# Two-layer hybrid encoder: seven-product pairs behind both standard parts, their products in another order, and two weight tiles a round split by an accumulating DMA

## The chip, the cores and the metric

One NeuronCore of one Trainium2 chip runs the whole program. The metric is device time in microseconds (us) from launch to end of one execution, lower is better. The kernel before takes 2075.16 us (median of 3 runs, 2074.29 to 2076.41).

## The reference, cut to what matters

```
SEQ, D_MODEL, D_FF, DEPTH = 256, 2048, 8192, 2           # batch 1, float32
for i in range(DEPTH):
    if i % 2 == 0: x = x + concat(conv(u), pool(u)) @ ev_w_out     # u = rms_norm(x) @ ev_w_in
    else:          x = x + fourier_mix(rms_norm(x)) @ od_w_out
    h = rms_norm(x, mlp_norm[i])
    x = x + jnp.square(jax.nn.relu(h @ mlp_w1[i])) @ mlp_w2[i]      # 2048 -> 8192 -> 2048
    g = jax.nn.sigmoid(rms_norm(x, ple_norm[i]) @ ple_w_gate[i])
    x = x + g * (p[i] @ ple_w_proj[i])
return rms_norm(x, final_norm)
```

The change lies in the line with `mlp_w1` and `mlp_w2` and in the order in which the products of `ple_w_gate` are added up.

## The kernel before, in words

**Split weights.** Every float32 product is made of three passes of a reduced-precision product: a value is held as hi + lo, and hi·hi, hi·lo and lo·hi are added up in PSUM (`PASSES_W_MOVES`). So every weight tile (128 x 2048 float32, 1 MB) is loaded by SyncE's queue into a buffer `raw` (4 of them), ScalarE writes its hi half into a buffer `hl` (L105), and VectorE writes lo = raw - hi beside it (L106). There are 4 `hl` buffers, used in turn, so the tile with number n can be split only when TensorE is through with the tile n-4. `Weights` holds the list of tiles in the order of their use; `run_ahead` splits up to three tiles ahead of the one in use. TensorE's and SyncE's instructions stand in the order in which the program names them; those of ScalarE and VectorE are ordered when the program is built, by a scheduler with priorities, and each engine then runs its own list strictly in that order.

**The MLP** (`mlp`, once a layer) goes in 8 rounds f. In each, `w1(q)` makes one block of 512 hidden columns from 4 tiles: of each tile it first does all products with the hi half (L580, 16 matmuls of 512 columns), then all with the lo half (L585, 16 of 256 columns). Its result is put through relu and square, split into `h` (L595 to L600) and combined into the sums `g` (L605 to L612). `w2(f, n)` is a standard product of two hidden blocks with two tiles of output columns n, added to x at its end (L366). `pair(f)` does the other half of the second product, output columns 0 to 1023, with seven products instead of eight (a Strassen-like scheme): for each of two blocks q the weights are two tiles, x and y, whose halves are split as they are or after an addition in place on VectorE (L102). The 14 products, each with 1024 columns of an `hl` tile, make 7 tiles; product by product they go into PSUM tiles a, b, c (1024 wide) and d (512), which VectorE adds to `sums` and to x (L649, L655, L657). After the last round `pair_end` combines `sums` into x (L662).

The order on TensorE in a round is w1(2f+2), w2(f,2), pair(f), w1(2f+3), w2(f,3); in the last round there is no w1, and `after.chunk(c)` brings parts of x, transposed by TensorE (L323) and split by ScalarE and VectorE (L262, L267), to the gate product that follows (`embed`, L345 with `ps_g`). `chunk` puts its transposes off by four steps of TensorE's work (`put_off`, `tick`).

The lines that set the order of the seven products before (weights, in `add_seven`):

```
parts += [
    [("split", (x, 0))], [("split", (x, q))],
    [("add", (x, 0), (y, 0)), ("split", (y, q))], [("split", (x, 0))],
    [("add", (y, 0), (y, q)), ("split", (y, 0))], [("add", (x, 0), (y, q)), ("split", (x, 0))],
    [("add", (x, 0), (x, q)), ("split", (x, 0))]]
```

Of the kernel before, what the change touches and what calls it, by code (L numbers as in the profile page):

```python
# [11 lines left out]
F32 = mybir.dt.float32  # L12
# [6 lines left out]
P = 128  # L19
# [11 lines left out]
RAW_BUFS = 4  # L31
RSQRT_MAGIC = float(0x5F3759DF)
# [10 lines left out]
class Weights:  # L43

# [24 lines left out]
    def add_seven(self, tiles):  # L69


        q, parts = 1024, []
        for x, y in tiles:
            x, y = self.source(x), self.source(y)
            parts += [
                [("split", (x, 0))], [("split", (x, q))],
                [("add", (x, 0), (y, 0)), ("split", (y, q))], [("split", (x, 0))],
                [("add", (y, 0), (y, q)), ("split", (y, 0))], [("add", (x, 0), (y, q)), ("split", (x, 0))],
                [("add", (x, 0), (x, q)), ("split", (x, 0))]]
# [15 lines left out]
    def divide(self, after_first=None):  # L95
# [3 lines left out]
        for i, (what, (r, c), other, w) in enumerate(steps):  # L99
# [6 lines left out]
            getattr(self.nc, lo).tensor_tensor(hl[:, 1, to], src, hl[:, 0, to].bitcast(F32), ALU.subtract)  # L106
# [32 lines left out]
def encoder(ctx: ExitStack, tc: tile.TileContext, a, out: bass.AP):  # L139
# [35 lines left out]
    def add_mlp(i):  # L175
        def w1(q):
            for c in range(4):
                ws.add(a["mlp_w1"][i, q, c])
# [102 lines left out]
    class Norm:  # L281
# [35 lines left out]
        def chunk(self, c):  # L317
# [9 lines left out]
            put_off(lambda: self.scale(c, turned))  # L327
# [228 lines left out]
    def mlp(i, norm, after):  # L556
# [64 lines left out]
        def pair(f):  # L621


            p15, p76, p23 = psum_mm(f"ps_s{i}_{f}a"), None, psum_mm(f"ps_s{i}_{f}b")
            p4 = sm_pool.tile([P, 512], F32, tag="sm", name=f"ps_s{i}_{f}d")
            k = 0
            for q in (2 * f, 2 * f + 1):
                h, g = hidden[q], forms[q]
                for what in range(7):
                    if k % 2 == 0:  # L630
                        w = ws.next()
                    if what == 4 and p76 is None:
                        p76 = psum_mm(f"ps_s{i}_{f}c")
                    out_ps = (lambda: p15[:, :512], lambda: p23[:, :512], lambda: p23[:, 512:], lambda: p15[:, 512:],
                              lambda: p76[:, :512], lambda: p76[:, 512:], lambda: p4)[what]()
                    for kt in range(2):
                        for m, (s, j) in enumerate(PASSES_W_MOVES):
                            act = (h[:, s, kt, :P], h[:, s, 2 + kt, :P], g[:, s, 3, kt], g[:, s, 0, kt],
                                   g[:, s, 2, kt], g[:, s, 1, kt], h[:, s, 2 + kt, P:])[what]
# [293 lines left out]
```

## Time and profile before

| | |
|---|---|
| median of 3 runs | 2075.16 us (2074.29 to 2076.41) |
| the profiled execution, its own time | 2070.65 us |
| its span, first to last instruction | 2068.9 us |
| mean granted clock of TensorE | 0.975 of full speed |
| TensorE, matmuls | 1977.0 us busy, 96% of the span |
| VectorE | 1564.3 us, 76% |
| ScalarE | 1039.6 us, 50% |
| GpSimd | 128.9 us, 6%, nearly all in the first layer's mixer |
| DMA | 377 MB, 182 GB/s over the span |

Shares of the span are averages over stages with different limits: the first 250 us are the mixer of layer 0, the two MLPs lie at about 252 to 990 us and 1213 to 1952 us, each followed by its gate product. Matmuls are pipelined and their ends are modelled, so TensorE's busy time counts some waiting; its pace is read from the starts of its instructions. PE is TensorE, DVE VectorE, ACT ScalarE, POOL GpSimd, SP SyncE; L106 is line 106 of the kernel.

### The profile page before, as it was taken

The numbers are of one execution on the slowest core, as the hardware profiler recorded it, in microseconds if no ns is written. First come the engines' busy times: TensorE is split into PE (matmuls) and PEld (weight loads), VectorE is DVE, ScalarE is ACT, GpSimd is POOL, SyncE is SP. The second block draws the span as 40 slices with busy tenths as digits, with TensorE's granted clock in tenths as the row PEclk, the third lists the DMA queues.
The fourth block names the chain that finished last, engine by engine and source line by source line (L and its number), as shares of the span: only waits on it lengthen the run. The fifth ranks groups of instructions, "written<-read, shape, count | busy, mean of one in ns | idle before, by whom it ended". The sixth has DMA issues, their size and how long they took to land.

```text
span 2068.9 us, 24040 instructions
## 1 busy us (share of the span) xinstructions
PE 1977.0 (96%) x9730; PEld 1668.3 (81%) x9730; DVE 1564.3 (76%) x1771; ACT 1039.6 (50%) x1087; POOL 128.9 (6%) x65
## 2 busy tenths in 40 slices
PE   8999999999999999998999999999999999999798
PEld 6888887878787787877789888787787878788686
DVE  7888768687787868779556567787868778787854
ACT  6345555445444545455454455545545445554543
POOL 3874000000000000000001000000000000000000
PEclk9999999999999999999999999999999999999999
DMA  8545554554536454464453554536364454635542
GB/s 330 192 170 191 206 188 168 187 203 143 224 140 227 152 214 183 143 223 162 152 183 135 183 183 146 224 139 240 137 231 169 159 209 146 222 135 203 182 164 108
DMA packets 55664, 377.43 MB, mean 182 GB/s; under 512 B 6384, under 2 KB 6528, under 8 KB 11648
## 3 DMA queue, kind: packets, MB, share of 16 engines
q1 hardware_dynamic: 55152, 374.82, 49.7%
q8 instruction: 76, 1.25, 0.2%
q10 hardware_dynamic: 144, 1.05, 0.1%
q14 instruction: 36, 0.29, 0.0%
q0 software_dynamic: 256, 0.02, 0.0%
HBM read 373.75 MB, written 2.10 MB: 182 GB/s over the span
## 4 chain that ended last, share of the span: by engine, by line
PE 69%; DVE 27%; issue 2%; ACT 2%; DMA 0%; ACTq 0%; SPq 0%
PE ps_h L580 21%; DVE hl L106 14%; PE ps_h L585 11%; PE ps_o L345 9%; PE ps_g L345 8%; DVE raw L102 7%; PE ps_od L345 4%; PE ps_in L345 4%; PE ps_out L345 3%; PE ps_pool L345 2%; ACT hl L105 2%; PE ps_outp L345 1%; PE ps_e L345 1%; DVE h L600 1%; DVE g L612 1%
## 5 line engine op out<-in xcount | busy, mean ns | idle before, releaser
L105 ACT ACTIVATE hl<-raw 128x2048 fp32r<-128x2048 f32 (+2 forms) x529 | 774.7, 1491 | 769.0 <-PE ps_h L585 315.8
L106 DVE TENSOR_TENSOR hl<-raw,hl 128x2048 fp32r<-128x2048 f32 (+3 forms) x501 | 865.5, 1744 | 381.5 <-ACT hl L105 379.8
L580 PE MATMUL ps_h<-xT_mlp,hl 128*128 128x512 f32 x2048 | 503.6, 399 | 0.0
L580 PEld LDWEIGHTS ps_h<-xT_mlp,hl 128*128 128x128 f32 x2048 | 391.1, 194 | 80.4
L345 PE MATMUL ps_o<-hl,h 128*128 128x512 f32 x1536 | 356.3, 391 | 0.0
L345 PEld LDWEIGHTS ps_o<-hl,h 128*128 128x128 f32 x1536 | 288.0, 189 | 58.7
L585 PEld LDWEIGHTS ps_h<-xT_mlp,hl 128*128 128x128 f32 x2048 | 262.6, 191 | 10.0
L585 PE MATMUL ps_h<-xT_mlp,hl 128*128 128x256 f32 x2048 | 266.0, 283 | 0.0
L345 PE MATMUL ps_g<-hl,xT_ple 128*128 128x512 f32 (+1 forms) x816 | 177.6, 377 | 0.0
L345 PEld LDWEIGHTS ps_g<-hl,xT_ple 128*128 128x128 f32 x816 | 146.4, 188 | 28.2 <-DVE hl L106 0.4
L106 POOL TENSOR_TENSOR hl<-raw,hl 128x2048 fp32r<-128x2048 f32 (+1 forms) x28 | 120.8, 4328 | 55.8 <-ACT hl L105 55.8
L345 PE MATMUL ps_in<-hl,xT_ev 128*128 128x512 f32 x384 | 90.8, 397 | 7.2 <-ACT hl L105 7.2
L442 DVE SCALAR_TENSOR_TENSOR acc<-vp,vT,acc 128x256 f32<-128x256 f32 x240 | 96.4, 481 | 0.1
L345 PEld LDWEIGHTS ps_in<-hl,xT_ev 128*128 128x128 f32 x384 | 73.4, 192 | 22.9 <-ACT hl L105 7.2
L345 PE MATMUL ps_od<-hl,f 128*128 128x512 f32 x384 | 88.1, 390 | 0.0
L595 ACT ACTIVATE relu<-ps_h 128x512 f32<-128x512 f32 x64 | 38.3, 598 | 96.4 <-PE ps_h L585 96.4
L345 PEld LDWEIGHTS ps_od<-hl,f 128*128 128x128 f32 x384 | 71.8, 188 | 14.8
L102 DVE TENSOR_TENSOR raw<-raw 128x1024 f32<-128x1024 f32 x64 | 78.0, 1219 | 0.7
L102 DVE TENSOR_TENSOR raw<-raw,raw 128x1024 f32<-128x1024 f32 x64 | 78.0, 1218 | 0.1
L782 POOL CAST top<-z 128x4 fp32r<-128x4 f32 x8 | 1.5, 189 | 931.7 <-DVE z L267 931.7
L596 DVE TENSOR_TENSOR relu<-ps_h,relu 128x512 f32<-128x512 f32 x64 | 42.7, 685 | 17.9 <-ACT relu L595 17.9
L611 ACT ACTIVATE g<-form 128x512 fp32r<-128x512 f32 x64 | 38.4, 623 | 24.4 <-DVE form L608 13.4
(283 smaller groups left out, 1716.6 us busy)
## 6 DMA issues: line engine op xcount, KB each, us to landing
raw<-in_mlp_w SPq DMA_DIRECT2D x256, 1024.0 KB, 4.9
raw<-in_ple_w_gate SPq DMA_DIRECT2D x32, 1024.0 KB, 5.0
raw<-in_w_in SPq DMA_DIRECT2D x20, 1024.0 KB, 5.0
raw<-in_ev_w_out SPq DMA_DIRECT2D x16, 1024.0 KB, 4.8
raw<-in_od_w_out SPq DMA_DIRECT2D x16, 1024.0 KB, 4.8
raw<-in_w_in SPq DMA_DIRECT2D x16, 256.0 KB, 6.3
raw<-in_ple_w_proj SPq DMA_DIRECT2D x8, 512.0 KB, 3.4
x<-in_x SPq DMA_DIRECT2D x2, 1024.0 KB, 7.9
```

The costliest lines, as they stand in the source:

```text
L102: self.nc.vector.tensor_tensor(src, src, self.raw[other[0]][:, other[1]:other[1] + w], ALU.add)
L105: self.nc.scalar.activation(hl[:, 0, to], src, AF.Copy)
L106: getattr(self.nc, lo).tensor_tensor(hl[:, 1, to], src, hl[:, 0, to].bitcast(F32), ALU.subtract)
L345: nc.tensor.matmul(ps[t][:, cols], lhsT=acts[:, s, kt, t * P:(t + 1) * P], rhs=w[:, m, kt * 512 + cols.start:kt * 512 + cols.stop], start= ...
L442: nc.vector.scalar_tensor_tensor(acc, src, cwT[:, ch, k:k + 1], acc, ALU.mult, ALU.add)
L580: nc.tensor.matmul(pss[p][:, e], lhsT=w[:, 0, ch], rhs=norm.xT[c][:, :, kt], start=c == 0 and kt == 0, stop=False, skip_group_check=True)
L585: nc.tensor.matmul(pss[p][:, e, 1], lhsT=w[:, 1, ch], rhs=norm.xT[c][:, 0, kt], start=False, stop=c == 3 and kt == 3, skip_group_check=True)
L595: nc.scalar.activation(r, pss[p][:, :, 1], AF.Copy)
L596: nc.vector.tensor_tensor(s, pss[p][:, :, 0], r, ALU.add)
L600: nc.vector.tensor_tensor(h[:, 1, e], s, h[:, 0, e].bitcast(F32), ALU.subtract)
L611: nc.scalar.activation(g[:, 0, to], src, AF.Copy)
L612: nc.vector.tensor_tensor(g[:, 1, to], src, g[:, 0, to].bitcast(F32), ALU.subtract)
```

## The change

Four things are done. (1) In a round `w2(f, 3)` goes ahead of `pair(f)`, so that both standard parts stand between w1(2f+2) and the pair, and w1(2f+3) behind it. In the last round the pair stays between w2(7,2) and w2(7,3). (2) The seven products go in the order `SEVEN`, another for the second block than for the first, with the additions where they are needed. (3) Of the w1 tiles of an even q from 2 on, c = 1 and 2 get their lo half without VectorE: ScalarE writes hi, then writes -hi into the lo half, and a DMA on GpSimd's queue reads the weights again from DRAM and adds them to it. That is 14 tiles a layer. (4) At a layer's end `pair_end` is put ahead of other work, `chunk(0)` and `chunk(1)` put their transposes off by 7 and 9 steps, and the gate product takes its four tiles in the order 2, 0, 1, 3.

```diff
+SEVEN = (1, 2, 5, 3, 6, 7, 4), (1, 5, 2, 6, 3, 4, 7)
...
     def add_seven(self, tiles):
         q, parts = 1024, []
-        for x, y in tiles:
+        for k, (x, y) in enumerate(tiles):
             x, y = self.source(x), self.source(y)
-            parts += [
...
+            made = {1: [("split", (x, 0))], 2: [("split", (x, q))], 3: [("split", (y, q))],
+                    5: [("add", (x, 0), (y, 0)), ("split", (x, 0))],
+                    6: [("add", (x, 0), (y, q)), ("split", (x, 0))],
+                    7: [("add", (y, 0), (y, q)), ("split", (y, 0))],
+                    4: [("add", (x, 0), (x, q)), ("split", (x, 0))]}
+            parts += [made[p] for p in SEVEN[k]]
...
             self.nc.scalar.activation(hl[:, 0, to], src, AF.Copy)
-            getattr(self.nc, lo).tensor_tensor(hl[:, 1, to], src, hl[:, 0, to].bitcast(F32), ALU.subtract)
+            if lo == "dma":
+                self.nc.scalar.activation(hl[:, 1, to], hl[:, 0, to].bitcast(F32), AF.Copy, scale=-1.0)
+                self.nc.gpsimd.dma_start(out=hl[:, 1, to], in_=self.srcs[r][0][:, c:c + w], accum_op=ALU.add)
+            else:
+                getattr(self.nc, lo).tensor_tensor(hl[:, 1, to], src, hl[:, 0, to].bitcast(F32), ALU.subtract)
...
             for c in range(4):
-                ws.add(a["mlp_w1"][i, q, c])
+                ws.add(a["mlp_w1"][i, q, c], lo="dma" if q % 2 == 0 and q and c in (1, 2) else "vector")
...
-            parts = [(a["ple_w_gate"][i, n, c], 2048) for c in range(4)]
+            parts = [(a["ple_w_gate"][i, n, c], 2048) for c in (2, 0, 1, 3)]
...
-            put_off(lambda: self.scale(c, turned))
+            put_off(lambda: self.scale(c, turned), steps)
...
         def pair(f):
...
+            def gather(p):
+                if p == 3:
+                    nc.vector.tensor_tensor(x[:, 0, :1024], tiles["b"], x[:, 0, :1024], ALU.add)
+                elif p == 4:
+                    nc.vector.tensor_tensor(x[:, 1, :512], tiles["d"], x[:, 1, :512], ALU.add)
+                elif p in (5, 7):
+                    ps, to = (tiles["a"], sums[:, :1024]) if p == 5 else (tiles["c"], sums[:, 1024:])
...
-            after.chunk(0)
+            after.chunk(0, 7)
...
-            after.chunk(1)
+            after.chunk(1, 9)
...
             if f < 7:
                 w1(2 * f + 2)
             w2(f, 2)
-            if f == 7:
-                after.chunk(2)
+            if f < 7:
+                w2(f, 3)
+                pair(f)
+                w1(2 * f + 3)
+                continue
+            after.chunk(2)
             pair(f)
-            if f == 7:
+            with tc.high_priority(offset=PRIO):
                 pair_end()
-            else:
-                w1(2 * f + 3)
             w2(f, 3)
-            if f == 7:
-                after.chunk(3)
+            after.chunk(3)
```

The list of tiles in `add_mlp` is put in the same order.

VectorE's list at the end of a pair, in round 3 of layer 0, before. The pair's tiles are hl115 to hl121, the next w1's hl122 to hl125; raw108 and raw109 are x and y of the second block, L106 makes lo, L102 is the addition in place.

```order
L102 TENSOR_TENSOR raw108_4519<-raw108_4519,raw109_4551 128x1024
L649 TENSOR_TENSOR x_81<-ps_s0_3b_4587,x_81 128x1024
L106 TENSOR_TENSOR hl121_4648<-raw108_4519,hl121_4648 128x1024
L655 TENSOR_TENSOR sums_119<-ps_s0_3a_4586,sums_119 128x1024
L102 TENSOR_TENSOR raw108_4519<-raw108_4519 128x1024
L106 TENSOR_TENSOR hl122_4669<-raw110_4625,hl122_4669 128x2048
L106 TENSOR_TENSOR hl121_4648<-raw108_4519,hl121_4648 128x1024
L106 TENSOR_TENSOR hl123_4687<-raw111_4646,hl123_4687 128x2048
```

The same place in the changed kernel, from the last product of the pair's fifth tile on: the pair's tiles are hl117 to hl123, the next w1's start at hl124; L115 makes lo, L107 is the addition.

```order
L107 TENSOR_TENSOR raw111_4620<-raw111_4620 128x1024
L115 TENSOR_TENSOR hl121_4675<-raw110_4588,hl121_4675 128x1024
L115 TENSOR_TENSOR hl122_4695<-raw111_4620,hl122_4695 128x1024
L107 TENSOR_TENSOR raw110_4588<-raw110_4588,raw111_4620 128x1024
L115 TENSOR_TENSOR hl122_4695<-raw110_4588,hl122_4695 128x1024
L115 TENSOR_TENSOR hl123_4716<-raw111_4620,hl123_4716 128x1024
L107 TENSOR_TENSOR raw110_4588<-raw110_4588 128x1024
L655 TENSOR_TENSOR sums_119<-ps_s0_3a_4661,sums_119 128x1024
L115 TENSOR_TENSOR hl123_4716<-raw110_4588,hl123_4716 128x1024
L647 TENSOR_TENSOR x_81<-ps_s0_3b_4668,x_81 128x1024
L115 TENSOR_TENSOR hl124_4738<-raw112_4693,hl124_4738 128x2048
```

Before, the whole lo of the next stage's first tile (hl122) stands ahead of the second half of the pair's last tile (hl121); now the pair's last tile (hl123) is finished ahead of hl124.

ScalarE's list while TensorE is in that next w1, before: hi halves (L105) of the tiles to come, then the copies of the w1's result (L595).

```order
L105 ACTIVATE hl126_4763<-raw114_4703 128x2048
L105 ACTIVATE hl127_4800<-raw115_4724 128x2048
L105 ACTIVATE hl128_4837<-raw116_4761 128x2048
L595 ACTIVATE relu_4873<-ps_h0_90_4722 128x512
L595 ACTIVATE relu_4881<-ps_h0_91_4723 128x512
```

Now, with hl128 to hl131 the tiles of the w1 after it (L110 writes hi, L112 writes -hi into the lo half, L606 copies the result):

```order
L110 ACTIVATE hl127_4795<-raw115_4754 128x2048
L110 ACTIVATE hl128_4832<-raw116_4772 128x2048
L110 ACTIVATE hl129_4869<-raw117_4793 128x2048
L112 ACTIVATE hl129_4869<-hl129_4869 128x2048
L110 ACTIVATE hl130_4907<-raw118_4830 128x2048
L112 ACTIVATE hl130_4907<-hl130_4907 128x2048
L606 ACTIVATE relu_4944<-ps_h0_90_4791 128x512
L606 ACTIVATE relu_4952<-ps_h0_91_4792 128x512
```

Two passes of ScalarE (L112) came in, and the two tiles' lo halves left VectorE's list; each L112 is followed by one DMA on GpSimd's queue.

## Rows read from the trace of the kernel before

**Rows 1.** Chain that ended last, the pieces of w2 in both layers: start, us, what.
```profile
375.53 10.91 PE ps_o L345 x48
...
835.35 10.91 PE ps_o L345 x48
927.51 21.80 PE ps_o L345 x96
...
1337.95 10.91 PE ps_o L345 x48
...
1890.06 21.80 PE ps_o L345 x96
```
**Rows 2.** Timeline of PE in round 4 of layer 0: start, us, instruction, count, [idle before].
```profile
667.38 3.82 PE L580 MATMUL ps_h<-xT_mlp,hl 128*128 128x512 f32 x16
...
672.94 3.82 PE L580 MATMUL ps_h<-xT_mlp,hl 128*128 128x512 f32 x16
...
684.08 11.07 PE L345 MATMUL ps_o<-hl,h 128*128 128x512 f32 x48
694.98 1.52 PE L641 MATMUL ps_s_4a<-hl,h 128*128 128x512 f32 x6
696.34 1.52 PE L641 MATMUL ps_s_4b<-hl,h 128*128 128x512 f32 x6
...
714.98 0.51 PE L641 MATMUL ps_s_4d<-hl,h 128*128 128x512 f32 x1 [1.92 <-ACT hl L105]
717.23 2.50 PE L641 MATMUL ps_s_4d<-hl,h 128*128 128x512 f32 x5 [1.75 <-DVE hl L106]
719.53 5.07 PE L580 MATMUL ps_h<-xT_mlp,hl 128*128 128x512 f32 x16
```
**Rows 3.** Stretches at that pair's end: us, busy PE, PEld, DVE, ACT, POOL, PEclk, DMA, GB/s.
```profile
712.80:717.20 4.40, 0.76 (x3) 0.19 (x1) 4.40 (x4) 3.93 (x3) 0.00 (x0) 0.79 0.15 61
...
719.50:722.00 2.50, 2.50 (x7) 1.98 (x6) 2.50 (x2) 0.91 (x1) 0.00 (x0) 0.50 0.97 387
```
**Rows 4.** Timeline of PE, the first w2 of layer 0.
```profile
319.72 10.62 PE L345 MATMUL ps_o<-hl,h 128*128 128x512 f32 x46
```
**Rows 5.** Timeline of DVE, the same round 4: start, us, instruction, count.
```profile
655.78 1.29 DVE L600 TENSOR_TENSOR h<-relu,h 128x512 fp32r<-128x512 f32 x2
656.98 0.42 DVE L605 TENSOR_TENSOR form<-relu 128x256 f32<-128x256 f32 x1
...
703.29 1.22 DVE L106 TENSOR_TENSOR hl<-raw,hl 128x1024 fp32r<-128x1024 f32 x1
704.43 1.22 DVE L102 TENSOR_TENSOR raw<-raw 128x1024 f32<-128x1024 f32 x1
```
**Rows 6.** Groups of instructions, shapes apart: count, busy us, mean ns, idle before.
```profile
L106 DVE TENSOR_TENSOR hl<-raw,hl 128x2048 fp32r<-128x2048 f32 x252 | 576.1, 2293 | 337.5 <-ACT hl L105 337.0
```
**Rows 7.** Timeline of ACT, the same pair and the w1 behind it.
```profile
705.68 1.06 ACT L105 ACTIVATE hl<-raw 128x1024 fp32r<-128x1024 f32 x1 [1.15 <-DVE raw L102]
...
726.55 1.92 ACT L105 ACTIVATE hl<-raw 128x2048 fp32r<-128x2048 f32 x1 [3.54 <-PE ps_h L585]
```
**Rows 8.** Timeline of PE at the end of layer 0's MLP, last pair to gate product.
```profile
949.14 1.52 PE L641 MATMUL ps_s_7a<-hl,h 128*128 128x512 f32 x6
...
954.58 1.03 PE L323 MATMUL tr_ple<-ident,x 128*128 128x128 f32 x8
...
982.39 1.76 PE L323 MATMUL tr_ple<-ident,x 128*128 128x128 f32 x7 [4.28 <-DVE x L662]
988.18 1.94 PE L323 MATMUL tr_ple<-ident,x 128*128 128x128 f32 x8 [4.04 <-DVE xT_ple L267]
...
1002.55 2.77 PE L345 MATMUL ps_g<-hl,xT_ple 128*128 128x512 f32 x11
```
**Rows 9.** The page, DMA issues: queue, count, KB each, median us to landing.
```profile
raw<-in_mlp_w SPq DMA_DIRECT2D x256, 1024.0 KB, 4.9
...
f<-tops POOLq DMA_DIRECT2D x8, 2.0 KB, 3.4
```

More of the change, by code (lines that the diff above doesn't have):

```diff
@@ L315, in scale, with chunk @@
                     divide_psum((xt[:, 0, 2 * h + j], xt[:, 1, 2 * h + j]), s[:, j], vT[:, k:k + 1])
-        def chunk(self, c):
+        def chunk(self, c, steps=4):
             def turned(h):
@@ L621, in pair, with psum @@
         def pair(f):
-            p15, p76, p23 = psum_mm(f"ps_s{i}_{f}a"), None, psum_mm(f"ps_s{i}_{f}b")
-            p4 = sm_pool.tile([P, 512], F32, tag="sm", name=f"ps_s{i}_{f}d")
+            tiles = {}
+            def psum(p):
+                key, half = {1: ("a", 0), 5: ("a", 1), 2: ("b", 0), 3: ("b", 1), 7: ("c", 0), 6: ("c", 1), 4: ("d", 0)}[p]
+                if key not in tiles:
+                    name = f"ps_s{i}_{f}{key}"
+                    tiles[key] = sm_pool.tile([P, 512], F32, tag="sm", name=name) if key == "d" else psum_mm(name)
+                return tiles[key][:, half * 512:(half + 1) * 512]
+            def gather(p):
[5 more added lines that the diff above has]
+                    ps, to = (tiles["a"], sums[:, :1024]) if p == 5 else (tiles["c"], sums[:, 1024:])
+                    if f == 0:
+                        nc.scalar.activation(to, ps, AF.Copy)
+                    else:
+                        nc.vector.tensor_tensor(to, ps, to, ALU.add)
             k = 0
@@ L645, in pair @@
                     k += 1
[L646 to L657 removed]
+                    if q % 2:
+                        gather(p)
         def pair_end():
@@ L720, in embed @@
                 w = [ws.next() for _ in range(4)]
-                for c in range(4):
-                    rows_product(pg[:1], norm.xT[c], range(4), c == 0, c == 3, w[c], (0,))
+                for k, c in enumerate((2, 0, 1, 3)):
+                    rows_product(pg[:1], norm.xT[c], range(4), k == 0, k == 3, w[k], (0,))
                 gated(0)
@@ L726, in embed @@
                     cols = slice(h * 256, (h + 1) * 256)
-                    for c in range(4):
-                        rows_product([None, pg[1 + h]], norm.xT[c], range(4), c == 0, c == 3, w[c], (1,), cols)
+                    for k, c in enumerate((2, 0, 1, 3)):
+                        rows_product([None, pg[1 + h]], norm.xT[c], range(4), k == 0, k == 3, w[k], (1,), cols)
                     gated(1, cols, [None, pg[1 + h]])
@@ L731, in embed @@
             else:
-                for c in range(4):
-                    rows_product(pg, norm.xT[c], range(4), c == 0, c == 3)
+                for k, c in enumerate((2, 0, 1, 3)):
+                    rows_product(pg, norm.xT[c], range(4), k == 0, k == 3)
                 rows_product(pe, pT, range(2), True, True)
```

34 lines of the change are left out of this document (8 added, 26 removed).

## The prediction

> **What bounds the kernel now.** The page's busy times come first: TensorE 96%, VectorE 76%, ScalarE 50%. They say that TensorE sets the time, but its busy time is modelled and holds waiting, so what a round costs is read from starts. In the chain of waits the pieces of w2 recur once a round [rows 1]: between 375.53 and 927.51 lie six rounds of layer 0, 552.0 us, and between 1337.95 and 1890.06 six of layer 1, 552.1 us, so a round takes 92.0 us. What it would take without a wait is read from the timeline of TensorE [rows 2]: a w1 tile 672.94 - 667.38 = 5.56 us, a w2 694.98 - 684.08 = 10.90, a product of the pair 696.34 - 694.98 = 1.36. Eight tiles, two w2 and 14 products make 44.5 + 21.8 + 19.0 = 85.3 us. **A round loses 6.7 us.** In round 0 one w2, the pair and one w1 should take 10.9 + 19.0 + 22.2 = 52.2 us and go from 319.72 [rows 4] to 375.53 [rows 1]: 55.8 us, a loss of 3.6.
>
> The loss lies in one place. The pair runs from 694.98 to 719.53, 24.55 us for 19.0, and the sixteen hi matmuls behind it take 5.07 us where others take 3.82 [rows 2]: 5.5 + 1.25. Of this 3.67 us are two waits of the pair's last product, 1.92 for ScalarE's hi and 1.75 for VectorE's lo. The rest is the clock: the granted clock is 0.79 in the stretch where TensorE was busy for 0.76 of 4.40 us, and 0.50 (1.2 of 2.4 GHz) in the one behind it [rows 3]. Why the last product is late stands in VectorE's list: a pair asks of it 14 lo halves, 8 additions and 4 gatherings of PSUM, nearly all 128 x 1024, one each 704.43 - 703.29 = 1.14 us [rows 5], some 29 us of work beside 19 us of TensorE. The four buffers bring a lead, which the list spends badly: a whole lo of 2.29 us [rows 6] for the next w1 stands ahead of the half tile that TensorE waits for.
>
> **The change: order of the round.** Count time from the pair's start, t = 0. Its first four tiles go into the buffers of the four w2 tiles, free at -16.4, -10.9, -5.5 and 0 (a w2 tile is half of 10.90), so three can be ready at the start, if VectorE gets there. From the end of w1 at -21.8 its list holds 4 relu steps, 2 lo of h, 2 of g and 2 additions to x at 0.6 each, 4 forms at 0.35, a whole lo (2.2), 6 half lo and 4 additions at 1.14 [rows 5, 6]: 6 + 1.4 + 2.2 + 11.4 = 21.0 us. It fits, with 0.8 to spare. From t = 0 on the new list reads: two additions to x (1.3, only now possible), two lo of the fourth tile (2.3), an addition, lo, addition, lo, lo, addition (6.8, to 10.4). The next lo needs a hi that ScalarE can make only from the sum, 1.06 us [rows 7], so VectorE waits 1.1; then lo, lo, addition, gathering, lo (5.7): **17.2 us**. TensorE asks for that last lo at the second matmul of the seventh tile, 6 x 2.72 + 0.2 = 16.5. It waits 0.7, with the handing over 0.9. The tiles before are in time: the fifth's lo at 8.2 for 10.9, the sixth's at 12.6 for 13.8. Without ScalarE's 1.1 nothing would be left of the wait, so 0 is the lower end; the upper end is the first rival. A wait of 0.9 us is a quarter of the 3.67 before which the clock fell, and I count no fall. Gain: 12 rounds x (6.7 - 0.9) = 69.6 us, 2 rounds 0 x (3.6 - 0.9) = 5.4 us.
>
> Next in line is the w1 behind the pair: its first lo is done at 17.2 + 1.1 + 2.2 = 20.5 and needed behind sixteen hi matmuls, at 19.9 + 3.65. Its load can start at about 2.5, when x of the first block is split for the last time, and lands 4.9 us later [rows 9]. Nothing there. The second w1 follows with no w2 between; half of its PSUM has to be freed within eight matmuls, 1.9 us, by a copy on ScalarE and one VectorE step of 0.6 each, for which both lists leave room: 0.
>
> **The change: lo by DMA.** 28 tiles lose 2.29 us of VectorE each, 64 us. On the path that is worth 0: these splits fall into the w1 stage, where VectorE follows ScalarE, and ScalarE idles 3.54 us a tile until TensorE frees a buffer [rows 7]. ScalarE's second pass, 1.92 us, goes into the same 3.54: 0. The DMA can start 0.2 + 2 x 1.92 = 4.0 us after the buffer is free, and its lo is asked for three tiles and sixteen matmuls later, 3 x 5.56 + 3.65 = 20.3: it has 16.3 us. No row shows an adding DMA. The nearest are a plain load of the same size, 4.9 us, and the smallest DMA of GpSimd's queue, 3.4 [rows 9]. Ends: 4.9, and two loads one after the other with that start on top, 13.2. I take the middle, 9, since it must read the weights and the tile it adds to, and its queue has nothing else to do. The second tile's DMA follows 5.56 us behind; if the two go one after the other it lands at 18 of 21.9. Hidden: 0. GpSimd's list has nothing else in the MLP; SyncE's queue gains, since these two raw buffers come free at ScalarE's pass.
>
> The Trainium skill (Collectives: The Full Stack, The bandwidth ceiling: the fold count and why AG ≠ RS ≠ AR) has a rule that speaks against this part: an add in a DMA fetches two sources for each piece that it writes, and runs at half the rate of a copy. By it the DMA would take some 9.8 us, an estimate from the load's 4.9, and two in a row would leave 2.3 us of their cover, still no cost; no run so far shows one.
>
> **The change: a layer's end.** From the last pair's start to the gate product's second tile TensorE takes 1002.55 - 949.14 = 53.4 us [rows 8] for a pair (19.0), a w2 (10.9), a gate tile (5.45) and four chunks of transposes of at most 1.0: 39.4. So 14 us are lost, 4.28 and 4.04 of them in waits for VectorE. In the new list, from the seventh tile's first lo to x's second block, stand 5 whole lo (11), three steps of 1.14 (3.4), six of 0.6 or less (3.6): 18 us. TensorE has two products and seven eighths of a w2 to do meanwhile, 12.3, so chunk 0 waits about 5.5; the pair's last tile waits 1.5 by the sum above, chunk 1 some 2.5 behind one more whole lo, and the clock costs about 2 again. That is 11.5 instead of 14: 2.5 us a layer, **5 us** in all, between 0 and 2 x 14.
>
> **Sum:** 69.6 + 5.4 + 5 = 80 us. The profiled execution (2070.65 us, its span and 1.75 around it) would go to 1990.7; it lies 4.5 under the median, from which the forecast is made: 2075.2 - 80 = **1995 us**.
>
> **Rivals.** *VectorE stays late.* The list before the pair fits by 0.8 us only, and two more of its lo follow an addition whose hi ScalarE may bring 1.1 us late. For it: all of this is in series, and what is over comes through in full in every round. Against it: two of the three such lo have other steps put between. 2 us more make the wait 2.9, 14 x 2 = 28 us less gained, 2023; if the clock falls too, as it cost 6.7 - 3.7 = 3 us so far, 2065. *The adding DMA lands too late*, the case that ends slower. Two in series delay TensorE by 2D - 21.9 for a DMA of D us; with the clock's 3 us the gain of 5.8 is used up at D = 12.4, without them at 13.9. At D = 15 a round loses 8.1 + 3 - 5.8 = 5.3 us: 14 x 5.3 - 5 = 69 over, 2144. For it: the upper end of 13.2 lies between these points. Against it: 15 us are three whole loads for one tile. *The change doesn't do what it says:* the DMA'd tiles relieve VectorE where it idles; by my sum that is so, and the time is the forecast's. *Nothing moves:* a new stall as large as the old one, for which no row speaks.
>
> **How the numbers follow.** Forecast 0.72, with a range of its own of 1974 (no wait left, 13 us, and 8 more at the layers' ends) to 2015 (1.4 us more of wait a round). VectorE late 0.15, DMA late 0.09, nothing moves 0.04. Faster by over 0.2%, about what a measurement of this kernel can tell from no change: 0.87; within it 0.04; slower 0.09. The range for 8 in 10 takes the forecast's and the nearer half of the first rival: 1974 to 2040.
>
> **What would show it.** Right: the pieces of w2 recur after about 86.2 us; the pair's last tile waits under 1.5 us for VectorE; the hi matmuls behind it take 3.8 us and the granted clock stays at full; 28 issues of hl on GpSimd's queue land in under 16 us and no lo matmul waits for them; the layer's end takes about 50 us. Wrong: a wait of 3 us or more at the seventh tile (first rival), or waits on DMA at the second or third tile of an even w1 (second).

## The result and the profile after

| | before | changed |
|---|---|---|
| median | 2074.72 us (4 runs, 2070.33 to 2076.41) | 2001.04 us (4 runs, 2000.22 to 2003.21) |
| ratio | 1 | 0.965, 95% interval 0.9633 to 0.9666 |
| profiled execution, its span | 2070.65, 2068.9 | 2001.12, 1998.9 |
| mean granted clock | 0.975 | 0.994 |

The changed kernel is 73.7 us faster by the medians and 69.5 by the profiled executions. The forecast was 1995 us, 80 less. The page of the changed kernel, its busy times:

```profile
PE 1948.5 (97%) x9730; PEld 1650.4 (83%) x9730; DVE 1500.6 (75%) x1743; ACT 1095.0 (55%) x1115; POOL 152.6 (8%) x93
```

VectorE lost its 64 us of lo, and its share barely fell, since the span fell with it. The shares say as little as before. The pieces of w2 in the chain answer to [rows 1]; both w2 of a round now stand together:

```profile
319.50 21.80 PE ps_o L356 x96
...
839.35 21.80 PE ps_o L356 x96
1245.31 21.80 PE ps_o L356 x96
...
1765.19 21.80 PE ps_o L356 x96
```

Six rounds take 839.35 - 319.50 = 519.85 us in layer 0 and 519.88 in layer 1: 86.64 a round, where it was 92.0 and the sum without a wait is 85.3. TensorE's timeline of round 3 in layer 0 shows the pair [rows 2 of before]; columns as there:

```profile
601.06 1.52 PE L668 MATMUL ps_s_3a<-hl,h 128*128 128x512 f32 x6
...
617.52 0.50 PE L668 MATMUL ps_s_3d<-hl,h 128*128 128x512 f32 x1
618.78 1.43 PE L668 MATMUL ps_s_3d<-hl,h 128*128 128x512 f32 x5 [0.76 <-DVE hl L115]
...
621.41 3.79 PE L591 MATMUL ps_h<-xT_mlp,hl 128*128 128x512 f32 x16
```

The pair takes 621.41 - 601.06 = 20.35 us, where it took 24.55. The two waits of 1.92 and 1.75 have become one of 0.76, and the hi matmuls behind it take 3.79: the clock no longer falls. VectorE's timeline says where the 0.76 comes from:

```profile
601.26 1.29 DVE L377 TENSOR_TENSOR x<-ps_o,x 128x512 f32<-128x512 f32 x2 [0.57 <-PE ps_o L356]
...
612.88 2.36 DVE L115 TENSOR_TENSOR hl<-raw,hl 128x1024 fp32r<-128x1024 f32 x2 [1.13 <-ACT hl L110]
615.16 1.22 DVE L107 TENSOR_TENSOR raw<-raw 128x1024 f32<-128x1024 f32 x1
616.29 1.22 DVE L655 TENSOR_TENSOR sums<-ps_s_3a,sums 128x1024 f32<-128x1024 f32 x1
617.50 1.23 DVE L115 TENSOR_TENSOR hl<-raw,hl 128x1024 fp32r<-128x1024 f32 x1
```

From the two additions to x to the last lo the list runs without a gap but for 1.13 us, in which VectorE waits for the hi of a sum, and ends 17.7 us behind the pair's start. TensorE has reached that lo's product by then. The 0.76 us are counted from the modelled end of the matmul before; by the starts the pair is 20.35 - 19.0 = 1.35 us longer than its products.

The gathering in this series (L655) is not what sets its end. In round 0 ScalarE does it, and VectorE waits for the hi of the last sum in its stead:

```profile
341.12 1.52 PE L668 MATMUL ps_s_0a<-hl,h 128*128 128x512 f32 x6
...
355.21 1.22 DVE L107 TENSOR_TENSOR raw<-raw 128x1024 f32<-128x1024 f32 x1
357.56 1.23 DVE L115 TENSOR_TENSOR hl<-raw,hl 128x1024 fp32r<-128x1024 f32 x1 [1.12 <-ACT hl L110]
```

There, too, the last lo ends 17.7 us behind the pair's start, and TensorE waits 0.76. What is left of the wait hangs on an addition, the hi of its sum and the lo, one after the other; the gathering only fills the time of that hi.

The adding DMAs, as busy time in the pair and in the w1 behind it (columns as in [rows 3]), and as issues on the page (us to landing, median):

```profile
601.06:621.41 20.35, 19.59 (x85) 15.69 (x84) 18.99 (x17) 12.10 (x11) 0.00 (x0) 1.00 0.47 172
621.41:643.65 22.24, 22.24 (x130) 19.68 (x128) 11.31 (x8) 13.58 (x8) 1.74 (x2) 1.00 0.98 336
```
```profile
raw<-in_mlp_w SPq DMA_DIRECT2D x256, 1024.0 KB, 5.2
...
hl<-in_mlp_w POOLq DMA_DIRECT2D x28, 1024.0 KB, 12.7
```

The 28 land after 8.6 to 14.6 us, and the DMA engines are busy 98% of the stretch in which they run. No row of TensorE waits for them. The end of layer 0's MLP, as in [rows 8]:

```profile
914.45 1.52 PE L668 MATMUL ps_s_7a<-hl,h 128*128 128x512 f32 x6
...
924.89 1.62 PE L668 MATMUL ps_s_7d<-hl,h 128*128 128x512 f32 x6 [1.21 <-DVE xT_ple L278]
...
951.62 1.75 PE L334 MATMUL tr_ple<-ident,x 128*128 128x128 f32 x7 [4.97 <-DVE x L679]
...
960.20 0.63 PE L334 MATMUL tr_ple<-ident,x 128*128 128x128 f32 x4 [3.00 <-DVE tot_ple L314]
...
967.18 16.58 PE L356 MATMUL ps_g<-hl,xT_ple 128*128 128x512 f32 x72
```

From the last pair's start to the second gate tile it takes 967.18 - 914.45 = 52.7 us, in layer 1 53.5, where it took 53.4. The end gained next to nothing.

### The profile page after: what moved, and what is told of

It is laid out like the page before. It is cut to its first block, busy times and chain, and to the rows that moved or that the text cites. A ratio compares the mean times of both kernels' runs of the same rounds, so it can differ in the third digit from the quotient of the medians.

```text
span 1998.9 us, 24141 instructions
## 1 busy us (share of the span) xinstructions
PE 1948.5 (97%) x9730; PEld 1650.4 (83%) x9730; DVE 1500.6 (75%) x1743; ACT 1095.0 (55%) x1115; POOL 152.6 (8%) x93
## 4 chain that ended last, share of the span: by engine, by line
PE 80%; DVE 17%; ACT 1%; issue 1%; DMA 0%; SPq 0%; ACTq 0%
PE ps_h L591 23%; PE ps_o L356 15%; PE ps_h L596 12%; DVE hl L115 9%; PE ps_g L356 9%; PE ps_od L356 4%; DVE raw L107 4%; PE ps_in L356 4%; PE ps_out L356 3%; PE ps_pool L356 2%; ACT hl L110 1%; PE ps_outp L356 1%; PE ps_e L356 1%; DVE sums L655 1%; DVE x L377 1%
## 5 line engine op out<-in xcount | busy, mean ns | idle before, releaser
L110 ACT ACTIVATE hl<-raw 128x1024 fp32r<-128x1024 f32 (+2 forms) x529 | 775.6, 1492 | 662.3 <-PE ps_h L596 218.4
L115 DVE TENSOR_TENSOR hl<-raw,hl 128x2048 fp32r<-128x2048 f32 (+2 forms) x473 | 797.5, 1710 | 222.2 <-ACT hl L110 220.6
L591 PE MATMUL ps_h<-xT_mlp,hl 128*128 128x512 f32 x2048 | 488.2, 390 | 0.0
L591 PEld LDWEIGHTS ps_h<-xT_mlp,hl 128*128 128x128 f32 x2048 | 377.4, 188 | 73.7
L596 PEld LDWEIGHTS ps_h<-xT_mlp,hl 128*128 128x128 f32 x2048 | 262.6, 191 | 9.9
L356 PE MATMUL ps_g<-hl,xT_ple 128*128 128x512 f32 (+1 forms) x816 | 181.8, 383 | 0.0
L115 POOL TENSOR_TENSOR hl<-raw,hl 128x2048 fp32r<-128x2048 f32 (+1 forms) x28 | 120.3, 4313 | 56.0 <-ACT hl L110 56.0
L113 POOL DMA_DIRECT2D hl<-in_mlp_w x28 | 24.5, 873 | 1252.8 <-ACT hl L112 1252.8
L107 DVE TENSOR_TENSOR raw<-raw,raw 128x1024 f32<-128x1024 f32 x64 | 77.9, 1218 | 0.5
L107 DVE TENSOR_TENSOR raw<-raw 128x1024 f32<-128x1024 f32 x64 | 77.7, 1217 | 0.1
L606 ACT ACTIVATE relu<-ps_h 128x512 f32<-128x512 f32 x64 | 38.2, 598 | 70.2 <-PE ps_h L596 70.2
L112 ACT ACTIVATE hl<-hl 128x2048 fp32r<-128x2048 f32 x28 | 53.6, 1915 | 0.9
## 6 DMA issues: line engine op xcount, KB each, us to landing
hl<-in_mlp_w POOLq DMA_DIRECT2D x28, 1024.0 KB, 12.7
```

Source lines behind the costliest of these rows:

```text
L107: self.nc.vector.tensor_tensor(src, src, self.raw[other[0]][:, other[1]:other[1] + w], ALU.add)
L110: self.nc.scalar.activation(hl[:, 0, to], src, AF.Copy)
L112: self.nc.scalar.activation(hl[:, 1, to], hl[:, 0, to].bitcast(F32), AF.Copy, scale=-1.0)
L113: self.nc.gpsimd.dma_start(out=hl[:, 1, to], in_=self.srcs[r][0][:, c:c + w], accum_op=ALU.add)
L356: nc.tensor.matmul(ps[t][:, cols], lhsT=acts[:, s, kt, t * P:(t + 1) * P], rhs=w[:, m, kt * 512 + cols.start:kt * 512 + cols.stop], start= ...
L591: nc.tensor.matmul(pss[p][:, e], lhsT=w[:, 0, ch], rhs=norm.xT[c][:, :, kt], start=c == 0 and kt == 0, stop=False, skip_group_check=True)
```

## The experiments

The first theory: the gain is the order of the round and nothing else; the DMA'd lo is worth nothing because VectorE idles where it would make it. Rivals: the DMA carries part of it, or the product order alone does. Times are medians, ratios are to the kernel before on the same chip.

| kernel | us | ratio, 95% interval | round, us |
|---|---|---|---|
| changed, all lo on VectorE | 1998.28 | 0.9647 (0.9631 to 0.9662) | 86.64 |
| changed, old layer end | 2005.21 | 0.9674 (0.966 to 0.9687) | 86.64 |
| before, w2(f, 3) moved alone | 2009.55 | 0.9695 (0.9682 to 0.9709) | 86.86, the first 86.46 |
| before, product order alone | 2053.11 | 0.9906 (0.9891 to 0.9921) | 90.3 |
| changed, one product order for both blocks | 1995.8 | 0.9632 (0.9616 to 0.9648) | 86.78, the first 85.37 |
| changed, one lo a round by DMA | 2000.57, one run | | 86.65 |
| changed, three lo a round by DMA | 2002.74 | 0.9662 (0.9648 to 0.9677) | 86.6 to 88.0 |
| changed, both w2 ahead of the last pair | 1992.62 | 0.9618 (0.9603 to 0.9634) | 86.67 |
| the last and one order together | 1987.84 | 0.9579 (0.9565 to 0.9593) | 86.78, the first 85.36 |
| changed, one lo of the pair on GpSimd | 2027.65 | 0.9771 (0.9755 to 0.9787) | 87.7 to 89.3 |
| control of it | 2003.61, one run | | 86.64 |
| all that was thought to help | 2018.1 | 0.9724 (0.9709 to 0.9738) | 87.7 to 89.3 |

**All lo on VectorE.**

```diff
-                ws.add(a["mlp_w1"][i, q, c], lo="dma" if q % 2 == 0 and q and c in (1, 2) else "vector")
+                ws.add(a["mlp_w1"][i, q, c])
```

> The changed kernel with the lo halves of all w1 tiles back on VectorE; all else as changed. My theory: the DMA'd tiles relieve VectorE where it idles (10.93 us before the relu steps in the changed kernel's trace), so they are worth nothing: within 3 us of the changed kernel's 2001 us, the pair's last tile still waits about 0.8 us, and the pieces of w2 still recur after 86.6 us. Rival: the 2 x 2.29 us a round that VectorE is spared carry over into the pair's lead; then a round is 1 to 4 us longer and the time 2015 to 2057 us.

Measured 1998.28 us, rounds of 86.64 and the same waits: VectorE got its 64 us back (1565.3 busy) and nothing became slower. The DMA part is worth nothing that these intervals can tell.

**The old layer end.** Part (4) of the change is undone.

```diff
-            parts = [(a["ple_w_gate"][i, n, c], 2048) for c in (2, 0, 1, 3)]
+            parts = [(a["ple_w_gate"][i, n, c], 2048) for c in range(4)]
...
-            after.chunk(0, 7)
+            after.chunk(0)
...
-            after.chunk(1, 9)
+            after.chunk(1)
...
-            with tc.high_priority(offset=PRIO):
-                pair_end()
+            pair_end()
...
```

> The changed kernel with the layer's end as before: pair_end without priority, chunks put off by four steps, gate tiles in the order 0 to 3. By the forecast's term the new end is worth 5 us, so 2006 us. By the changed kernel's trace it is worth nothing: from the last pair's start to the second gate tile 52.7 and 53.5 us against 53.4 before, so 2001 us within 3.

Measured 2005.21 us, 4.2 more by the medians and 4.1 by the spans (2003.0 and 1998.9). The rounds are the same, and the stretch from the last pair to the second gate tile takes 56.0 us in layer 0 and 55.7 in layer 1. So part (4) does bring its few microseconds, but from 56.0 and not from the 53.4 of before: something else in the change had made the end longer. It is not the last pair, which takes 21.8 us here; what stands behind it grew, from 31.4 us before (971.18 to 1002.55) to 34.2 (936.29 to 970.47).

**The move alone, in the kernel before.**

```diff
             w2(f, 2)
-            if f == 7:
-                after.chunk(2)
+            if f < 7:
+                w2(f, 3)
+                pair(f)
+                w1(2 * f + 3)
+                continue
+            after.chunk(2)
             pair(f)
-            if f == 7:
-                pair_end()
-            else:
-                w1(2 * f + 3)
+            pair_end()
             w2(f, 3)
-            if f == 7:
-                after.chunk(3)
+            after.chunk(3)
```

The list of tiles is put in the same order.

> The kernel before with one thing changed: in rounds 0 to 6 the second standard part goes ahead of the pair. Products in the old order, no DMA'd lo, old ends. VectorE's list here still has the whole lo of the next w1 ahead of the pair's last half tile. If the lead is what counts: VectorE has the last lo done about 18.4 us after the pair's start, asked for at 17.9, a wait of 0.5 to 1, a round of 86 to 87 us, 1997 to 2008 us in all. If the order of the list is what counts (2.2 us of a whole lo and 1.9 of a whole hi ahead of the last half tile): a wait of 3 us or more, half clock after it, a round of 90 us or more, 2045 us or more.

Measured 2009.55 us, 64 less than before on the same chip (2073.5): most of the gain comes from the order of the round. The run with the old layer end, on the same chip, has the product order and the DMA'd lo on top of the move and takes 2005.21 us, so these two add 4.3. The round and its wait (86.86 and 0.84 us) are what the theory of the lead expected; the time is 1.6 us above its range, and the layer ends, which it did not count, got longer. The end takes 56.1 us (916.33 to 972.42 in layer 0) where it took 53.4, and TensorE's timeline shows where most of that was lost:

```profile
916.33 1.52 PE L643 MATMUL ps_s_7a<-hl,h 128*128 128x512 f32 x6
...
928.32 2.90 PE L643 MATMUL ps_s_7d<-hl,h 128*128 128x512 f32 x6 [2.76 <-DVE xT_ple L269]
...
940.90 5.62 PE L347 MATMUL ps_o<-hl,h 128*128 128x512 f32 x24
```

The same two places in the kernel before, whose last pair starts at 949.14 [rows 8]:

```profile
959.21 1.62 PE L641 MATMUL ps_s_7d<-hl,h 128*128 128x512 f32 x6 [0.84 <-DVE xT_ple L267]
...
971.18 5.61 PE L345 MATMUL ps_o<-hl,h 128*128 128x512 f32 x24
```

The last pair takes 24.57 us, where it took 22.04, and its first product in d waits 2.76 us for VectorE in place of 0.84. Before, w2(6, 3) and w2(7, 2) stood directly ahead of it; now there is a w1 ahead and one w2, so the last pair lost the lead that all the others won.

**The product order alone, in the kernel before:** part (2), with the rounds and the ends as they were.

```diff
+SEVEN = (1, 2, 5, 3, 6, 7, 4), (1, 5, 2, 6, 3, 4, 7)
...
-                for what in range(7):
+                for p in SEVEN[q % 2]:
```

> The kernel before with one thing changed: the order of the seven products. Places of the standard parts, splits and ends as before. Its list has the whole lo behind the pair's last half tile. If the lead is what counts: the last lo comes 20 to 21 us after the pair's start and is asked for at 16.5, a wait of about 4 us and half clock after it as before, no gain or little: 2055 to 2080 us. If the order of the list is what counts: the wait goes, 2000 to 2020 us.

Measured 2053.11 us; rounds of 89.5 and 91.1 in turn. That is just below the range expected if the lead counts, and far above the one expected if the order of the list does. The waits did not go: in round 4 of layer 0 TensorE waits 0.30, 0.76, 0.55 and 1.40 us, 3.0 in place of 3.67. The order alone brings some 20 us, and beside the move, as the 4.3 us above show, it has little left to bring.

**One product order for both blocks.**

```diff
-SEVEN = (1, 2, 5, 3, 6, 7, 4), (1, 5, 2, 6, 3, 4, 7)
+SEVEN = (1, 2, 5, 3, 6, 7, 4), (1, 2, 5, 3, 6, 7, 4)
```

> The changed kernel with one edit: the second block's seven products go in the same order as the first's, 1 2 5 3 6 7 4. Theory: the wait that is left in a pair, 0.8 us, is VectorE finishing its last lo at 17.7 us of the pair for a product that TensorE asks for at about 16.9. With product 4 last, TensorE asks for that lo one product later (some 1.3 us), but the built order of VectorE then puts the next w1's whole lo (2.2 us) ahead of the last half lo: the wait becomes 0.5 to 0.7 us and the time 1993 to 1999. Rival, the order of the second block is what keeps the pair fed: the wait comes back at 2 us or more, a clock fall behind it, 2020 to 2060.

The time came out as expected, 1995.8 us (span 1992.9 against 1998.9), for another reason. The rounds did not get shorter (86.78, only the first 85.37; wait 0.76: a whole lo for the next w1 now stands ahead of the last half lo, as foreseen). The gain lies where nothing was expected, at the layer ends, 4.4 us at the first and 1.1 at the second. TensorE's timeline of the first:

```profile
926.64 1.80 PE L668 MATMUL ps_s_7d<-hl,h 128*128 128x512 f32 x6 [2.75 <-DVE xT_ple L278]
...
939.52 9.69 PE L356 MATMUL ps_o<-hl,h 128*128 128x512 f32 x42
...
950.74 0.98 PE L334 MATMUL tr_ple<-ident,x 128*128 128x128 f32 x7 [1.42 <-DVE x L679]
...
962.92 16.59 PE L356 MATMUL ps_g<-hl,xT_ple 128*128 128x512 f32 x72
```

The pair itself takes 3.0 us more than in the changed kernel (24.85), but from its end to the second gate tile it is 23.4 in place of 30.9: chunk 0 waits 1.42 us for x in place of 4.97, and the granted clock behind that wait is 1.00 (950.74 to 962.92) where it was 0.79. VectorE's list behind the last product, first the changed kernel, then this one:

```profile
932.33 6.76 DVE L115 TENSOR_TENSOR hl<-raw,hl 128x1024 fp32r<-128x1024 f32 x4
...
941.34 2.29 DVE L115 TENSOR_TENSOR hl<-raw,hl 128x2048 fp32r<-128x2048 f32 x1
943.54 1.22 DVE L655 TENSOR_TENSOR sums<-ps_s_7c,sums 128x1024 f32<-128x1024 f32 x1
944.68 2.28 DVE L115 TENSOR_TENSOR hl<-raw,hl 128x2048 fp32r<-128x2048 f32 x1
946.88 0.68 DVE L679 TENSOR_TENSOR sums<-sums 128x512 f32<-128x512 f32 x1
947.48 2.28 DVE L115 TENSOR_TENSOR hl<-raw,hl 128x2048 fp32r<-128x2048 f32 x1
949.68 0.68 DVE L679 TENSOR_TENSOR x<-x,sums 128x512 f32<-128x512 f32 x1
```
```profile
944.26 1.22 DVE L655 TENSOR_TENSOR sums<-ps_s_7c,sums 128x1024 f32<-128x1024 f32 x1
...
945.99 0.68 DVE L679 TENSOR_TENSOR sums<-sums 128x512 f32<-128x512 f32 x1
946.59 2.29 DVE L115 TENSOR_TENSOR hl<-raw,hl 128x2048 fp32r<-128x2048 f32 x1
948.79 0.69 DVE L679 TENSOR_TENSOR x<-x,sums 128x512 f32<-128x512 f32 x1
```

From the gathering of c to the sum that chunk 0 needs two whole lo of 2.28 us stand in the list of the changed kernel, and one in this one. That is a part of it: VectorE has that sum 34.8 us behind the pair's start in place of 35.9. The rest of the 3.55 us by which the wait is shorter is on TensorE's side, which comes there 2.5 us later. From the last pair's start to the second gate tile it is 48.2 us in place of 52.7. All waits in that stretch fall from 9.5 us to 6.5 together; the rest of the 4.5 is the clock. It stays up behind the shorter wait, where 12.2 us pass to the second gate tile in place of 15.6, and falls in the pair instead, to 0.71 from 926.6 to 932.4. The longer pair comes from products 5 and 2: a run further down that exchanges these two alone (the control of the run with GpSimd) has it, too, 24.6 us, and 53.6 for the whole stretch. The gain comes from the rest of the order, 3 ahead of 6 and 7 ahead of 4.

**One and three lo by DMA.**

```diff
-                ws.add(a["mlp_w1"][i, q, c], lo="dma" if q % 2 == 0 and q and c in (1, 2) else "vector")
+                ws.add(a["mlp_w1"][i, q, c], lo="dma" if q % 2 == 0 and q and c == 1 else "vector")
```

With three it reads `c in (1, 2, 3)`.

> The changed kernel with only one lo of an even w1 by DMA (c = 1; c = 2 goes back to VectorE). Theory: the adding DMA takes 12.4 and 14.1 us in the changed kernel because two of them and the plain loads share the DMA engines, busy 98% of that stretch; alone it lands in 8 to 10.5 us. Rival, an adding DMA is that slow by itself: it still takes 12 us or more. The time is the changed kernel's, 1998 to 2002, in both cases.

> The changed kernel with three lo halves of an even w1 by DMA (c = 1, 2, 3). The theory says that the DMAs cost nothing as long as they land inside their cover of 16.3 us. The DMA engines were busy 98% of that stretch with two, so a third lands at 16 to 20 us: TensorE waits 0 to 3 us for it in most of the 14 even w1, and the plain loads behind it come later too: 2001 to 2030. If the third lands within 16 us too, the time is 1998 to 2003. Rival, that the second DMA was at its edge already: all three late, over 2050.

With one, the DMA lands after 8.1 to 11.9 us, median 10.9, between the two theories: the second one beside it costs some 2 us of the 12.7. The larger part of the distance to a plain load's 4.9 stays. It was not alone even then, for with one adding DMA, too, the engines are busy 99% of that stretch (622.15 to 644.39), with the plain loads. But on the page of the changed kernel the packets of GpSimd's queue take 7.3% of the engines' span for 29.4 MB, those of the plain loads 51.0% for 374.8 MB: 1.8 times as long for a byte, and 1.9 and 1.8 times with one and with three a round. So much of it goes with the adding DMA, however many there are. With three, the longest takes 15.2 us, inside the cover of 16.3, and the median stays at 12.7. All that TensorE's lo matmuls then wait is 1.6 us in two places, and the twelve rounds together take 3.0 us more than in the changed kernel:

```profile
L596 PE MATMUL ps_h<-xT_mlp,hl 128*128 128x256 f32 x2048 | 266.6, 283 | 1.6 <-DMA hl<-in_mlp_w 1.6
```

The third did not land at 16 to 20, so the upper part of what was expected was a miss; 2002.74 us is within the runs of the changed kernel. The rival that the second DMA stood at the edge is out.

**Both w2 ahead of the last pair.** In the last round w2(7, 3) goes ahead of the pair, chunk 2 is turned while w2(7, 3) runs and chunk 3 while the pair does, and the gate product takes these two first.

```diff
             w2(f, 2)
...
             after.chunk(2)
+            w2(f, 3)
+            after.chunk(3, finish=False)
             pair(f)
             with tc.high_priority(offset=PRIO):
                 pair_end()
-            w2(f, 3)
-            after.chunk(3)
...
-                for k, c in enumerate((2, 0, 1, 3)):
+                for k, c in enumerate((2, 3, 0, 1)):
```

> The changed kernel with another layer end: both w2 of the last round stand ahead of the last pair, as in the other rounds, and the gate product takes its four tiles in the order 2, 3, 0, 1, so that chunks 2 and 3 of x are there while the last pair is put together. Theory: the last pair lost the lead that two w2 directly ahead of it give, and chunks 0 and 1 wait for VectorE's additions behind the pair; with the lead back and two gate tiles as cover each layer's end gives back 4 to 7 us, 1987 to 1993. Rival: the series of VectorE's additions behind the last product sets the end whatever stands around it, 1999 to 2003.

Measured 1992.62 us, as expected; but neither of the two reasons is seen as it was given. In TensorE's list of waits the sums over both layers are now

```profile
PE ps_s_7d L666 <- DVE xT_ple L276: 4.5, 2, 2.7
PE tr_ple L332 <- DVE x L677: 2.6, 2, 1.3
```

(us in total, times, longest). The last pair waits more, not less (1.86 and 2.67 where it was 1.21 and 1.22), for VectorE's split of the eight transposes that lie in it; there are eight in the changed kernel, too, and why the split comes later is not shown. Chunk 0 waits 1.3 us in place of 4.97, but the two gate tiles are no longer cover than w2 was: from the pair's end to chunk 0's transposes TensorE has 9.8 us of work (950.35 to 960.14), where it had 10.4. It is VectorE that has the sum sooner:

```profile
951.55 2.28 DVE L115 TENSOR_TENSOR hl<-raw,hl 128x2048 fp32r<-128x2048 f32 x1
...
957.28 2.29 DVE L115 TENSOR_TENSOR hl<-raw,hl 128x2048 fp32r<-128x2048 f32 x1
959.48 0.69 DVE L677 TENSOR_TENSOR x<-x,sums 128x512 f32<-128x512 f32 x1
```

It ends 9.8 us behind the pair's end and not 14.1: two whole lo stand ahead of it in place of three (941.34, 944.68 and 947.48 in the changed kernel), and no half lo are left over, which there ran until 939.1, 2.8 us past the pair's end. So what pays is that VectorE has less to do between the pair and the sum.

**Both ends together**, the edits of the two runs in one kernel, the version that beats both kernels.

> The changed kernel with the layer end of e8_new_ends and the product order of e5_same_order together. e5's gain lay in the layer ends, not in the rounds: with product 4 last, only half as much of PSUM is to be gathered behind the last product, and chunk 0 waited 1.4 us for x in place of 5.0. If the two act on different parts of the end they add up: 1987 less 5 for e5 and 9 for e8 from 2001, so 1985 to 1989. Rival, both shorten the same wait: 1991 to 1995, e8 alone.

Measured 1987.84 us, ratio 0.9579, an interval that does not meet that of the changed kernel: 13 us less than its median. From the seventh w2 piece to the next layer's first the changed kernel takes 1245.31 - 839.35 = 406.0 us, with one order 401.6, with the w2 ahead 402.7, with both 400.6 (838.60 to 1239.19); from the last piece to the end 233.7, 232.6, 227.5 and 225.4. The gains over both layers are 5.5 and 9.5 us alone and 13.7 together: they nearly add up.

**One lo of the pair on GpSimd, and its control.** This tries to take away the 0.76 us that a pair still waits.

```diff
-SEVEN = (1, 2, 5, 3, 6, 7, 4), (1, 5, 2, 6, 3, 4, 7)
+SEVEN = (1, 2, 5, 3, 6, 7, 4), (1, 2, 5, 6, 3, 4, 7)
...
+            if k == 1:
+                made[7][1] = ("split_pool", (y, 0))
...
-                getattr(self.nc, lo).tensor_tensor(hl[:, 1, to], src, hl[:, 0, to].bitcast(F32), ALU.subtract)
+                getattr(self.nc, "gpsimd" if what == "split_pool" else lo).tensor_tensor(hl[:, 1, to], src, hl[:, 0, to].bitcast(F32), ALU.subtract)
```

> The changed kernel with one lo fewer in VectorE's series at a pair's end: the lo of the second block's product 7 is made on GpSimd, and products 6 and 3 of that block change places, so that VectorE's list has the addition for product 4 directly behind the lo of product 6. Theory: the 0.8 us that a pair still waits are this series of addition, hi and lo, and one step of 1.14 us less takes the wait away: rounds of 85.4 to 85.9 us in place of 86.64, time 1986 to 1992. Rival, the wait has another cause, or GpSimd's lo comes late or slows VectorE: rounds of 86.6 or more, 2000 or more.

> The changed kernel with products 6 and 3 of the second block in exchanged places and every lo where it was, the control of e10_pool_lo: VectorE's list keeps its length, so the wait stays at 0.6 to 0.9 us, rounds at 86.5 to 86.8, time 1998 to 2003. If the exchange alone does it, the rounds fall to 85.9 or less.

The theory's way out failed: 2027.65 us. As the edit shows, both runs exchange products 5 and 2 of the second block, and not 6 and 3 as was written ahead of them; 6 and 3 stand as in the changed kernel. The control has the changed kernel's rounds (86.64), its wait of 0.76 and 2003.61 us, so it is not the exchange. VectorE's and GpSimd's timelines of the same pair:

```profile
619.47 1.23 DVE L117 TENSOR_TENSOR hl<-raw,hl 128x1024 fp32r<-128x1024 f32 x1 [1.12 <-ACT hl L112]
620.73 3.30 DVE L109 TENSOR_TENSOR raw<-raw 128x1024 f32<-128x1024 f32 x1
...
625.15 1.22 DVE L117 TENSOR_TENSOR hl<-raw,hl 128x1024 fp32r<-128x1024 f32 x1
```
```profile
620.47 2.47 POOL L117 TENSOR_TENSOR hl<-raw,hl 128x1024 fp32r<-128x1024 f32 x1 [57.13 <-ACT hl L112]
```

The addition that starts 0.26 us behind GpSimd's lo takes 3.30 us in place of 1.22, until 1.1 us after GpSimd is through, and so it does in all fourteen pairs of rounds 0 to 6: the two do not run side by side. It is the very addition on which the last hi and lo hang, so TensorE waits 1.03 us for that hi and again 0.76 for the lo. In some rounds the clock falls behind these waits, and the round takes 89.3 us, in others it doesn't: 87.7.

The Trainium skill (SBUF — State Buffer, SBUF: two separate sides) says that a VectorE operation with two inputs in SBUF and a GpSimd operation that reads SBUF exclude each other for the whole instruction: the one that starts first has the shared port, and the other stands still. The trace agrees, 2.47 us of GpSimd and then 1.1 of the addition.

**All that was thought to help:** the two ends (product 4 last in the last round alone) and the lo on GpSimd.

```diff
-                for p in SEVEN[q % 2]:
+                for p in SEVEN[q % 2 if f < 7 else 0]:
...
```

> The changed kernel with all that helped: the layer end of e8_new_ends, product 4 last in the last round alone, and the rounds of e10_pool_lo. If the parts add up as measured or expected one by one (9 from e8, 5 from e5, 10 to 14 from e10): 1973 to 1980. If e10 brings nothing: 1985 to 1990.

Measured 2018.1 us, outside both ranges, which took it that GpSimd's lo brings something or nothing. The layer ends' gain is there (10.2 us less than in the changed kernel over both), and GpSimd's lo takes more than that back: the twelve rounds take 25.4 us more.

## Why the prediction was right, and where it was off

- **Order of the round: right, and it is the gain.** The move alone brings 64 us. The two waits of 3.67 us became one of 0.76 with no half clock behind, as worked out. The round fell to 86.64 where 86.2 was forecast: 0.9 was taken for what is left, and by the starts it is 1.35. VectorE's last lo ends at 17.7 us and not at 17.2, since the list starts 0.2 behind the pair and its steps take 0.3 more than the sum has, and each 0.1 comes through. That the sum has the gathering as a step in series is wrong by round 0, where the hi of the last sum takes its place; the two are about equally long, so the sum comes out right there by luck. Twelve rounds gave 12 x 5.36 = 64.3 us of the 69.6. From an MLP's first matmul to its last pair it was 697.5 and 699.3 us and is 663.2 and 663.3, 70.3 less in the two layers together: so the two rounds 0, with what stands ahead of them, gave 6.0, where 5.4 was forecast.
- **VectorE stays late, nothing moves:** not what happened. That the series before the pair fits by only 0.8 us did no harm (VectorE waits 0.57 us for TensorE at its end); what is left is the series behind the pair's start, and the GpSimd run shows how directly it passes on what comes late there.
- **Lo by DMA: worth 0, as predicted,** shown by leaving it out. Its price was mis-sized, 9 us where 12.7 were measured, so that at least half of the 28 lie above the rival's lower limit of 12.4, and the longest above its upper one of 13.9. It was no cost because these limits were worked out for two DMAs one after the other. They overlap: the longest of two takes 14.6 us, of three 15.2, both below the cover of 16.3. The Trainium skill (Collectives: The Full Stack, The bandwidth ceiling: the fold count and why AG ≠ RS ≠ AR) tells of the adding step of a collective that it reads two sources and runs at about half the rate of the copying step. Carried over to this DMA it gave an estimate of 9.8 us; measured were 10.9 with one DMA a round, so it has the direction and nearly the size here, and the measurement decides.
- **A layer's end: the term that failed.** Forecast was 2.5 us a layer, measured are 0.7 and -0.1. The waits add up as forecast: 1.5 + 5.5 + 2.5 = 9.5, and 1.21 + 0.28 + 4.97 + 3.00 = 9.5 measured in layer 0. In part that is luck: the 1.5 stood for the last tile's wait for its lo, which did not come, and the 1.21 is another wait, of the first block's product 4 for VectorE's split of the transposes. What was mis-sized is "the clock costs about 2 again": the 52.7 us hold 39.4 of work and 9.5 of waits, so 3.8 are left, and in layer 1, with 10.0 of waits, 4.1. It was more than 2 before the change, too: there the waits are 0.84, 0.70, 1.00, 4.28 and 4.04, and 53.4 - 39.4 - 10.9 = 3.1 are left. The windows show the clock at 0.79 behind the long wait:

```profile
951.60:967.20 15.60, 12.58 (x54) 10.43 (x54) 11.03 (x28) 9.46 (x21) 0.00 (x0) 0.79 0.37 143
```

 In layer 1 the second gate tile, too, takes 17.96 us in place of 16.6. Behind the number lies an oversight that the experiments name: the end was taken as if only part (4) touched it. The move took the last pair's lead (2.5 us longer in the move's own run). With the new product order that pair is as short as before, but 2.8 us more stand behind it with the old end, and the run with one order for both blocks gives back 4.4 and 1.1 us. Part (4) brought 3.3 and 2.2 us against these.
- **The sum.** From the profiled execution 1990.7 was forecast, and it took 2001.1: 75.0 - 70.3 = 4.7 us of the difference lie in the rounds, the rest at the ends and in layer 1's gate product. The median of before was 4.5 above its profiled run, which is why 1995 looks nearer to 2001.0.

Left open: why an adding DMA takes twice a plain one's time, and whether the pair's last 0.76 us can be had in every round without GpSimd. In the run with one order round 0 has no such wait and takes 85.37 us; there ScalarE does the gathering, which in that list stands in VectorE's way. No run has ScalarE do it in the other rounds.

## What to carry to other kernels

Where one stage asks more of a helper engine than its own length gives, put all stages that ask little of it directly ahead: that is worth more than taking work off the helper where it idles anyway. When an order is good for every round, cost the last round by itself, for it loses what the others win, and what stands behind it reads its result. When a wait gets shorter, look which of the two sides moved, and what the clock does behind it. Before work goes to an idle engine, look whether it shares something with the engine that is to be relieved.

## What was not expected of the hardware

- An adding DMA of 1 MB from GpSimd's queue took 10.9 us (median, one a round) and 12.7 (two or three), beside 4.9 to 5.8 for plain loads of the same weights in the same runs; a second one beside it adds 1.8 us to the median, a third nothing.
- A VectorE addition of 1.22 us took 3.30 when a GpSimd subtraction of 2.47 us began 0.26 us ahead of it, in all fourteen pairs of rounds 0 to 6.
- In the run with GpSimd's lo the same two waits, 1.03 or 1.04 and 0.76 us, brought TensorE's clock down in some rounds and not in others. The windows of two such rounds differ in the clock, 0.98 and 1.00, and by 1.6 us (below). In the run with both w2 ahead of the last pair the clock was 0.71 in the 5.8 us behind a wait of 1.86 (layer 0), and 1.00 in the 5.8 behind one of 2.67 (layer 1).

```profile
496.72:586.03 89.31, 87.52 (x437) 74.21 (x437) 68.46 (x64) 49.42 (x44) 4.24 (x3) 0.98 0.64 212
586.03:673.75 87.72, 85.92 (x438) 73.09 (x437) 68.37 (x64) 49.44 (x44) 4.23 (x3) 1.00 0.64 216
```
